# Long differential-attention rows: the first part of the probabilities corrected by two accumulating matmuls with diagonal matrices

## The chip, the cores and the metric

The kernel runs on one core of a Trainium2 chip. TensorE (PE) does the matmuls and the transposes, VectorE (DVE), ScalarE (ACT) and GpSimd (POOL) work element by element, SyncE (SP) issues most of the DMAs. The metric is the device time of one execution in microseconds.

## The reference

One inference step of a two-layer decoder with four parallel mixers in each layer. The change touches the differential attention of the prompt: 2048 tokens, 4 heads, two softmax maps per head whose difference weighs the values.

```python
SEQ = 2048
DEPTH = 2
A_HEADS = 4
Q_BLOCK = 128

def _diff_attend(q1, q2, k1, k2, v, qpos, kpos, lam):
    scale = q1.shape[-1] ** -0.5
    visible = kpos[None, :] <= qpos[:, None]

    def probs(q, k):
        s = jnp.einsum('bqhd,bkhd->bhqk', q.astype(F32), k.astype(F32)) * scale
        return jax.nn.softmax(jnp.where(visible, s, NEG_BIG), axis=-1)

    p = probs(q1, k1) - lam * probs(q2, k2)
    return jnp.einsum('bhqk,bkhd->bqhd', p, v.astype(F32))
...
    o_a = (_rms_norm(o_a, attn_norm_g[l]) * (1.0 - lam_init)).reshape(Bn, T, GROUP_W)
    o_a = o_a * jax.nn.silu(ag.astype(F32))
...
    mixed = jnp.concatenate([o_a, o_b, o_c, o_d], -1).astype(dt) @ w_out[l]
    y = _layer_norm(ALPHA * x + gate[:, None, :] * mixed, ln_g[l], ln_b[l]).astype(dt)
```

## The kernel before

In each layer the projections and the three other mixers come first, then the attention, block by block (tiles 0 to 3, 4 to 7, 8 to 11, 12 and 13, 14 and 15 of 128 queries), with the output projection of finished tiles (`out_tile`, L1326, matmuls L1373 to L1375, 48 per tile) placed among the attention's work.

`attention` (L630) loads keys and queries of one head, and for each tile calls `attn_probs` for it and then `attn_value` for the tile ahead of it, so values run one tile behind. A tile with its head is called a head-tile here.

`attn_probs` (L663) works for the two maps m = 0 and 1 in pieces of up to 1024 keys. For each piece PE makes the scores S (L678, the mask L680), DVE the negated row maximum (L682; in a second piece L684 takes the smaller of the two), ACT the exp into a buffer P with the row sum beside it (L686). Rows of more than 1024 keys (tiles 8 to 15) have two pieces. The first was made with its own maximum, so it needs a correction: a column per map, `col(m, 5)`, from a small exp on ACT (L691). Then DVE forms `r`, the ratio of the two maps' sums times −lambda (L697, L698), and the two maps are joined: P1 + r·P2 for the last piece (L712), and for the first piece of a long row P1·col(0,5) + P2·col(1,5)·r, in three steps: L702 forms the product of the two columns (DVE), L706 scales P2 by it (ACT), L707 scales P1 and adds (DVE). The maps have buffers of their own, P1 five and P2 three.

`attn_value` (L715) turns the joined probabilities in groups of four blocks of 128 keys: four transposes on PE (L725) into a PSUM tile T (of two), a copy to `ph` on ACT (L727, two buffers), four value matmuls (L730) that accumulate in the PSUM tile X. After the last tile of a block X is copied to `asb` (a buffer of its own), turned by L741 and normalised with rows of two `ms` buffers.

The order in which each engine issues its work is not the order of the code. A scheduler that simulates the program sets it, with priorities given by `prio`; any change of an instruction's kind or buffers can therefore move others. The instructions that it moves are shown with the change below.

Of the kernel before, what the change touches and what calls it, by code (L numbers as in the profile page):

```python
# [9 lines left out]
F32 = mybir.dt.float32  # L10
# [4 lines left out]
AF = mybir.ActivationFunctionType  # L15
ALU = mybir.AluOpType
# [8 lines left out]
P = 128  # L25
# [43 lines left out]
def hymba_step_kernel(  # L69
# [9 lines left out]
    nc = tc.nc  # L79
# [9 lines left out]
    RW = TG + NS  # L89
    NB = TG // 512  # L90

    KN = dict(zs=5, ms=2, os=4, NK=5, NMW=8, APO='o k p2 h p1 v v0 op q', ORD0='g10 n1 g2 b4 g4 n1', ORD1='g8 n2',
              NPH=2, NP1=5, NP2=3, LEAD=1, KD0=0, KD1=1, LO0=2, LO1=2, ZIP=0, WF=0, RUN=1, QB=0, RB=0, RC=0, RD=1, RS=1,
              RA=0, RO=0, GP=1, CI=1, CS=0, MO=0, PT=300, PSA=0, PN=1000, PB=0, PG=0, PD=1000, PBV=0, PCZ=0, PGB=0,
              POUT=-500, PATT=0, PMOD=0, PW=0, PAV=0, PDZ=3000, PQK=500, PSL=0, PSLD=0, PPR=0, PPB=0, OT=1, GO=0, DO=0,
              EP2=0, ECB=0, EPH=0, EAS=0, EAV=0, EDV=0, EOH=0, EOL=1, EOT=1, ESH=0, ESL=1, EQK=1, EDN=1, EAN=1, EDB=1,
# [15 lines left out]
    NK, NMW, NPH, NP1, NP2, LEAD = (KN[k] for k in ('NK', 'NMW', 'NPH', 'NP1', 'NP2', 'LEAD'))  # L112
    APO, ORD0, ORD1 = (KN[k].split() for k in ('APO', 'ORD0', 'ORD1'))
# [20 lines left out]
    def nm(s):  # L134
        uid[0] += 1
        return f"{s}_{uid[0]}"
# [14 lines left out]
    def st(tag, dt=F32):  # L151

        return stp.tile([P, 512], dt, tag=tag, name=nm(tag), bufs=NST[tag])
# [46 lines left out]
    ident = cst[:, C_ID:C_ID + 128]  # L200
# [462 lines left out]
    def attn_probs(qi, qt, kst, l1, Lx, ap):  # L663
# [32 lines left out]
        r = col(0, 7)  # L696
        nc.vector.reciprocal(r, lt2)  # L697
        nc.vector.scalar_tensor_tensor(r, lt1, Lx.nlam, r, op0=ALU.mult, op1=ALU.mult)  # L698
        for pc, n in enumerate(sizes):
            p1, p2 = p1s[pc], p2s[pc]  # L700
            if pc == 0 and npc > 1:
                nc.vector.tensor_tensor(col(1, 7), col(1, 5), r, ALU.mult)  # L702
                if KN['EP2']:
                    nc.gpsimd.tensor_scalar(p2[:, :n], p2[:, :n], col(1, 7), None, op0=ALU.mult)
                else:
                    nc.scalar.activation(p2[:, :n], p2[:, :n], AF.Copy, scale=col(1, 7))  # L706
                nc.vector.scalar_tensor_tensor(p1[:, :n], p1[:, :n], col(0, 5), p2[:, :n], op0=ALU.mult, op1=ALU.add)  # L707
            elif n <= KN['ECB'] * P:
                nc.scalar.activation(p2[:, :n], p2[:, :n], AF.Copy, scale=r)
                nc.gpsimd.tensor_tensor(p1[:, :n], p1[:, :n], p2[:, :n], ALU.add)  # L710
            else:
                nc.vector.scalar_tensor_tensor(p1[:, :n], p2[:, :n], r, p1[:, :n], op0=ALU.mult, op1=ALU.add)  # L712
        return p1s

    def attn_value(qi, pm, vst, acc, ls, j4, nt, hd, act, Lx, l, ap):  # L715

# [1 line left out]
        hs = slice(hd * 64, (hd + 1) * 64)  # L718
        for c in range(0, nk, 4):
            n = min(4, nk - c)  # L720
            p1 = pm[c // 8]
            o = (c % 8) * P
            pt = Tt()
            for j in range(n):
                nc.tensor.transpose(pt[:, j * P:(j + 1) * P], p1[:, o + j * P:o + (j + 1) * P], ident)  # L725
            ph = ap.h.tile([P, 4, P], F32, tag="ph", name=nm("ph"), bufs=NPH)
            (nc.vector.tensor_copy if n <= KN['EPH'] else nc.scalar.copy)(ph[:, 0:n].rearrange("p k q -> p (k q)"), pt[:, 0:n * P])  # L727
            for j in range(n):
                e = (c + j) % 2
                nc.tensor.matmul(acc[e * 64:(e + 1) * 64, j4 * P:(j4 + 1) * P], vst[c // 4][:, j, hs], ph[:, j, :],  # L730
                                 start=(c + j < 2), stop=(c + j >= nk - 2), tile_position=(0, e * 64))
        if nk == 1:
            nc.vector.memset(acc[64:128, 0:P], 0.0)
        if j4 < nt - 1:
            return
        asb = ap.o.tile([P, 512], F32, tag="asb", name=nm("asb"), bufs=1)
        cpy('EAS', asb[:, 0:nt * P], acc[:, 0:nt * P])

        pt = Tt()
# [835 lines left out]
```

## Time and profile before

| | |
|---|---|
| median of 3 runs | 3167.21 us (3165.14 to 3172.83) |
| the profiled execution | 3160.83 us |
| its span | 3159.1 us, mean granted TensorE clock 0.951 |
| PE busy | 2828.0 us, 90% of the span |
| DVE busy | 2235.2 us, 71% |
| ACT busy | 1162.9 us, 37% |
| POOL busy | 960.8 us, 30% |
| long rows, layer 0 and layer 1 | 1182 to 1572 and 2712 to 3108 us |

The shares are means over the whole span. The edited lines run in the two stretches of long rows alone, a quarter of the time, so tables of single stretches say more than the page. A row of such a table gives a stretch, its length, and for each engine busy time and count of instructions, then the granted clock of TensorE (1.00 is full speed), the share of the DMA engines and their GB/s. A matmul's own duration includes its way through the array; the next one starts earlier, so a group's time from start to start is what one costs.

### The profile page before, as it was taken

What the parts mean: (1) busy time and instruction counts of PE and PEld (TensorE: products, weight loads), DVE (VectorE), ACT (ScalarE), POOL (GpSimd) and SP (SyncE); (2) the same over time, 40 slices, a digit from 0 to 9 for tenths busy, and PEclk for the clock granted to TensorE, in tenths of its full rate; (3) what the DMA queues carried; (4) which work ended last, traced back from release to release, by engine and by line L of the source; (5) the groups of instructions that cost most, each with busy time, mean ns of one, the idle gap of its engine ahead of it and who ended that gap; (6) DMA issues with size and microseconds to landing.
All of it is one profiled execution on the core that took longest, in us unless ns stands there. A gap on an engine that the chain in (4) does not pass through costs nothing. (4 is left out here: it accounts for less than half of the span.)

```text
span 3159.1 us, 55749 instructions
## 1 busy us (share of the span) xinstructions
PE 2828.0 (90%) x20888; PEld 2254.7 (71%) x20888; DVE 2235.2 (71%) x5280; ACT 1162.9 (37%) x2452; POOL 960.8 (30%) x1061
## 2 busy tenths in 40 slices
PE   5999989898999798888979999999999988997986
PEld 3888876788876566656668888767888856665665
DVE  2567883367583788879956678833676749898897
ACT  3212223211112666666641112232110146567663
POOL 3344364312011233404253344552120031332232
PEclk8999999899999899989989999999999988998998
DMA  6433544323555754446453335444334355444652
GB/s 237 147 128 108 173 146 154 108 92 128 174 180 203 184 133 112 118 112 166 122 197 111 122 119 192 140 139 124 117 120 140 117 166 123 129 118 108 158 155 67
DMA packets 323263, 441.31 MB, mean 140 GB/s; under 512 B 58704, under 2 KB 207734, under 8 KB 315811
## 3 DMA queue, kind: packets, MB, share of 16 engines
q1 hardware_dynamic: 316850, 420.97, 44.0%
q0 software_dynamic: 6144, 16.79, 1.8%
q8 instruction: 165, 2.70, 0.4%
q14 instruction: 104, 0.84, 0.1%
HBM read 295.80 MB, written 142.05 MB: 139 GB/s over the span
## 5 line engine op out<-in xcount | busy, mean ns | idle before, releaser
L525 PE MATMUL z<-hh,wh 128*128 128x512 f32 (+1 forms) x1440 | 528.4, 367 | 17.1 <-DVE zs L195 9.1
L527 PE MATMUL z<-hh,wl 128*128 128x512 f32 (+1 forms) x1440 | 522.1, 363 | 0.0
L526 PE MATMUL z<-hl,wh 128*128 128x512 f32 (+1 forms) x1440 | 518.6, 360 | 0.0
L516 PE MATMUL z<-wh,hh 128*128 128x256 f32 (+1 forms) x1360 | 399.9, 294 | 16.0 <-ACT wh L110 4.3
L686 ACT ACTIVATE P<-S,stt 128x1024 f32<-128x1024 f32 (+7 forms) x384 | 332.7, 868 | 182.1 <-DVE stt L682 120.0
L518 PE MATMUL z<-wh,hl 128*128 128x256 f32 (+1 forms) x1360 | 394.7, 290 | 0.0
L517 PE MATMUL z<-wl,hh 128*128 128x256 f32 (+1 forms) x1360 | 393.9, 290 | 0.6 <-POOL wl L172 0.6
L682 DVE TENSOR_REDUCE stt<-S 128x1 f32<-128x1024 f32 (+7 forms) x384 | 344.0, 904 | 64.2 <-PE S L680 48.7
L1026 DVE SCALAR_TENSOR_TENSOR acc<-glu,cw,acc 128x512 f32<-128x512 f32 x480 | 378.0, 834 | 3.3
L525 PEld LDWEIGHTS z<-hh,wh 128*128 128x128 f32 x1440 | 275.7, 191 | 80.1 <-issue 14.4
L527 PEld LDWEIGHTS z<-hh,wl 128*128 128x128 f32 x1440 | 275.5, 191 | 44.7 <-issue 7.0
L526 PEld LDWEIGHTS z<-hl,wh 128*128 128x128 f32 x1440 | 275.7, 191 | 42.7 <-issue 6.3
L678 PE MATMUL S<-K,Q 128*128 128x512 f32 (+3 forms) x640 | 229.2, 430 | 77.1 <-ACT P L686 61.6
L516 PEld LDWEIGHTS z<-wh,hh 128*128 128x128 f32 (+1 forms) x1360 | 262.3, 193 | 25.9 <-issue 5.7
L517 PEld LDWEIGHTS z<-wl,hh 128*128 128x128 f32 (+1 forms) x1360 | 261.9, 193 | 4.9 <-issue 2.6
L518 PEld LDWEIGHTS z<-wh,hl 128*128 128x128 f32 (+1 forms) x1360 | 261.5, 192 | 2.3 <-issue 0.3
L172 POOL TENSOR_TENSOR wl<-raw,wh 128x512 fp32r<-128x512 f32 x112 | 150.8, 1362 | 256.5 <-ACT wh L110 218.2
L1373 PE MATMUL z<-woh,zs 128*128 128x512 f32 (+1 forms) x480 | 202.7, 422 | 24.0 <-ACT zs L110 15.1
L1375 PE MATMUL z<-woh,zs 128*128 128x512 f32 (+1 forms) x480 | 200.2, 417 | 10.0 <-POOL zs L172 9.8
L730 PE MATMUL X<-ph,V 128*64 128x128 f32 x2176 | 196.1, 294 | 10.4 <-ACT ph L727 9.8
L678 PEld LDWEIGHTS S<-K,Q 128*128 128x128 f32 x640 | 114.9, 204 | 122.1 <-ACT P L686 90.0
L725 PE MATMUL T<-cst,P 128*128 128x128 f32 x1088 | 189.2, 302 | 13.3 <-DVE P L707 8.8
(374 smaller groups left out, 5410.5 us busy)
## 6 DMA issues: line engine op xcount, KB each, us to landing
wp<-wh SPq DMA_DIRECT2D x28, 1024.0 KB
wp<-wl SPq DMA_DIRECT2D x28, 1024.0 KB
wh<-wp SPq DMA_DIRECT2D x56, 512.0 KB
wl<-wp SPq DMA_DIRECT2D x56, 512.0 KB
K<-kh SPq DMA_DIRECT2D x224, 128.0 KB
K<-kl SPq DMA_DIRECT2D x224, 128.0 KB
mw<-in_w_ada_dram SPq DMA_DIRECT2D x24, 1024.0 KB
raw<-in_w_in_dram SPq DMA_DIRECT2D x64, 256.0 KB
```

The lines of the kernel that those rows point to most:

```text
L516: nc.tensor.matmul(ps, hh[:, k, tok:tok + M], wh[:, k, :], start=(k == 0), stop=False)
L517: nc.tensor.matmul(ps, hh[:, k, tok:tok + M], wl[:, k, :], start=False, stop=False)
L518: nc.tensor.matmul(ps, hl[:, k, tok:tok + M], wh[:, k, :], start=False, stop=(k == KT - 1))
L525: nc.tensor.matmul(ps, wh[:, k, ms], hh[:, k, c0:c0 + n], start=(k == 0), stop=False)
L526: nc.tensor.matmul(ps, wh[:, k, ms], hl[:, k, c0:c0 + n], start=False, stop=False)
L527: nc.tensor.matmul(ps, wl[:, k, ms], hh[:, k, c0:c0 + n], start=False, stop=(k == KT - 1))
L678: nc.tensor.matmul(s[:, o:o + w], qt[:, m, :], kst[pc * 2 + o // 512][:, m, 0:w], start=True, stop=not diag)
L682: nc.vector.tensor_reduce(col(m, pc), s[:, :n], AX.X, ALU.max, negate=True)
L686: nc.scalar.activation(p[:, :n], s[:, :n], AF.Exp, bias=col(m, pc), scale=1.0, accum_out=l1 if m == 0 and npc == 1 else col(m, 2 + pc))
L1026: nc.vector.scalar_tensor_tensor(av, src(j), Lx.cw[:, c, j:j + 1], av, op0=ALU.mult, op1=ALU.add)
L1373: nc.tensor.matmul(po[0:M], a, wh[:, k, :], start=(i == 0), stop=False)
L1375: nc.tensor.matmul(po[0:M], b, wh[:, k, :], start=False, stop=(i == KT - 1))
```

## The change

For the first piece of a long row the three passes L702, L706 and L707 are gone. Instead `attn_probs` makes two 128x128 diagonal matrices from the identity, one with col(0,5) and one with col(1,5)·r on the diagonal, in a buffer `dg` (two of them), and hands P1, P2 and `diag` to `attn_value`. There each transpose of the first eight blocks becomes two fp32 matmuls into the same part of T: P1's block times the first diagonal matrix, P2's block times the second, accumulated. Since a block is the stationary operand, the product comes out turned as before. The first piece of P2 is thus read by PE and no longer by ACT and DVE. `asb` becomes an `ms` buffer, which leaves room for the matrices. A branch for very short rows that no row took is gone too.

```diff
-    KN = dict(zs=5, ms=2, os=4, NK=5, NMW=8, APO='o k p2 h p1 v v0 op q', ORD0='g10 n1 g2 b4 g4 n1', ORD1='g8 n2',
+    KN = dict(zs=5, ms=2, os=4, NK=5, NMW=8, APO='o k p2 h p1 v v0 op q dg', ORD0='g10 n1 g2 b4 g4 n1', ORD1='g8 n2',
...
+        diag = None
         for pc, n in enumerate(sizes):
             p1, p2 = p1s[pc], p2s[pc]
             if pc == 0 and npc > 1:
-                nc.vector.tensor_tensor(col(1, 7), col(1, 5), r, ALU.mult)
-                if KN['EP2']:
-                    nc.gpsimd.tensor_scalar(p2[:, :n], p2[:, :n], col(1, 7), None, op0=ALU.mult)
-                else:
-                    nc.scalar.activation(p2[:, :n], p2[:, :n], AF.Copy, scale=col(1, 7))
-                nc.vector.scalar_tensor_tensor(p1[:, :n], p1[:, :n], col(0, 5), p2[:, :n], op0=ALU.mult, op1=ALU.add)
-            elif n <= KN['ECB'] * P:
-                nc.scalar.activation(p2[:, :n], p2[:, :n], AF.Copy, scale=r)
-                nc.gpsimd.tensor_tensor(p1[:, :n], p1[:, :n], p2[:, :n], ALU.add)
+                diag = ap.dg.tile([P, 2, P], F32, tag="dg", name=nm("dg"), bufs=2)
+                nc.vector.tensor_scalar(diag[:, 0], ident, col(0, 5), None, op0=ALU.mult)
+                nc.vector.tensor_scalar(diag[:, 1], ident, col(1, 5), r, op0=ALU.mult, op1=ALU.mult)
             else:
                 nc.vector.scalar_tensor_tensor(p1[:, :n], p2[:, :n], r, p1[:, :n], op0=ALU.mult, op1=ALU.add)
-        return p1s
+        return p1s, p2s, diag
...
-            p1 = pm[c // 8]
+            p1s, p2s, diag = pm
             o = (c % 8) * P
             pt = Tt()
             for j in range(n):
-                nc.tensor.transpose(pt[:, j * P:(j + 1) * P], p1[:, o + j * P:o + (j + 1) * P], ident)
+                ks, js = slice(o + j * P, o + (j + 1) * P), slice(j * P, (j + 1) * P)
+                if diag is not None and c < 8:
+                    for m, p in enumerate((p1s[0], p2s[0])):
+                        nc.tensor.matmul(pt[:, js], p[:, ks], diag[:, m], start=(m == 0), stop=(m == 1))
+                else:
+                    nc.tensor.transpose(pt[:, js], p1s[c // 8][:, ks], ident)
...
-        asb = ap.o.tile([P, 512], F32, tag="asb", name=nm("asb"), bufs=1)
+        asb = st("ms")
```

In the rows of the order below, a name with its numbers is one tile of that name, and what stands behind the arrow is read. After the change the code's lines are shifted: L724 are the paired matmuls, L726 the transposes that stay (L725 before), L731 the value matmuls (L730), L742 the turning of the head's sum (L741), L708 the last piece's combination (L712), L1355 the turning in `out_tile` (L1354) and L1374 to L1376 the output projection (L1373 to L1375).

PE, in a long head-tile of layer 0, before the change: scores of one tile, transposes and value matmuls of the tile ahead (T the transposed blocks, X the value sum).

```order
L680 MATMUL S_1893_12986<-cmaskb_110,identb_108 128x128
L741 MATMUL T_1865_12882<-cst_81,asb_1864_12880 128x64 x4
L1354 MATMUL z_2089_13859<-cst_81,os_2085_13854 128x128 x4
L730 MATMUL X_1874_12914<-ph_1885_12957,V_1189_10171 64x128 x4
L725 MATMUL T_1888_12974<-cst_81,P_1853_12822 128x128
L725 MATMUL T_1886_12963<-cst_81,P_1851_12815 128x128 x4
L678 MATMUL S_1895_12995<-K_1844_12789,Q_1847_12804 128x512
L678 MATMUL S_1895_12995<-K_1845_12794,Q_1847_12804 128x512
L730 MATMUL X_1874_12914<-ph_1887_12968,V_1406_10944 64x128 x4
L725 MATMUL T_1899_13016<-cst_81,P_1877_12920 128x128 x4
L730 MATMUL X_1874_12914<-ph_1889_12976,V_1707_12206 64x128
```

The P tiles that L725 reads here are joined ones: one transpose per block, in groups of four, with score and value matmuls between the groups.

PE, the corresponding part of a long head-tile of layer 0 after the change (dg the diagonal matrices, P read from both maps in turn).

```order
L731 MATMUL X_1884_12981<-ph_1898_13043,V_1407_10947 64x128 x4
L731 MATMUL X_1884_12981<-ph_1900_13051,V_1708_12209 64x128
L678 MATMUL S_1906_13070<-K_1853_12848,Q_1856_12863 128x512
L678 MATMUL S_1906_13070<-K_1854_12853,Q_1856_12863 128x512
L724 MATMUL T_1911_13091<-dg_1894_13015,P_1887_12987 128x128
L678 MATMUL S_1908_13076<-K_1855_12858,Q_1856_12863 128x384
L680 LDWEIGHTS identb_108
L680 MATMUL S_1908_13076<-cmaskb_110,identb_108 128x128
L724 MATMUL T_1911_13091<-dg_1894_13015,P_1891_13002 128x128
L724 MATMUL T_1911_13091<-dg_1894_13015,P_1887_12987 128x128
L724 MATMUL T_1911_13091<-dg_1894_13015,P_1891_13002 128x128
```

The eight transposes of a first piece are sixteen matmuls now, two per block with P of the one map and of the other, and the next tile's scores (L678) stand among them.

DVE, at the last long tile of layer 1 before the change, from the reciprocal to the first piece's combination (stt the columns, the small rows in between belong to normalisations).

```order
L697 RECIPROCAL stt_5208_32157<-stt_5208_32157 128x1
L179 TENSOR_SCALAR smai_5203_32139<-sma_5201_32134 128x2
L189 SCALAR_TENSOR_TENSOR smoa_5290_32524<-smoa_5290_32524,smoy_5289_32523 128x1
L698 SCALAR_TENSOR_TENSOR stt_5208_32157<-ls_5179_32041,nlam_2721_16683,stt_5208_32157 128x1
L181 TENSOR_SCALAR smay_5204_32140<-smai_5203_32139 128x2
L190 SCALAR_TENSOR_TENSOR smoy_5289_32523<-smoa_5290_32524,smoy_5289_32523 128x1
L702 TENSOR_TENSOR stt_5208_32157<-stt_5208_32157 128x1
L712 SCALAR_TENSOR_TENSOR P_5212_32170<-P_5216_32186,stt_5208_32157,P_5212_32170 128x1024
L183 TENSOR_TENSOR smaa_5205_32141<-sma_5201_32134,smay_5204_32140 128x2
L1385 SCALAR_TENSOR_TENSOR smo_5287_32520<-omv_5285_32517,smoy_5289_32523 128x1
L707 SCALAR_TENSOR_TENSOR P_5210_32162<-P_5210_32162,stt_5208_32157,P_5214_32178 128x1024
```

L702 and L707 enclose the last piece's combination L712, and L706 runs on ACT between them.

DVE, at the same tile after the change.

```order
L693 SCALAR_TENSOR_TENSOR stt_5273_32660<-stt_5273_32660 128x1
L189 SCALAR_TENSOR_TENSOR smaa_5270_32644<-smaa_5270_32644,smay_5269_32643 128x2
L697 RECIPROCAL stt_5273_32660<-stt_5273_32660 128x1
L190 SCALAR_TENSOR_TENSOR smay_5269_32643<-smaa_5270_32644,smay_5269_32643 128x2
L698 SCALAR_TENSOR_TENSOR stt_5273_32660<-ls_5243_32536,nlam_2754_16943,stt_5273_32660 128x1
L183 TENSOR_TENSOR smaa_5270_32644<-sma_5266_32637,smay_5269_32643 128x2
L706 TENSOR_SCALAR dg_5282_32695<-cst_81,stt_5273_32660 128x128
L708 SCALAR_TENSOR_TENSOR P_5277_32673<-P_5281_32689,stt_5273_32660,P_5277_32673 128x1024
```

The pass over 1024 columns that read P twice (L707) and the column product ahead of it (L702) are gone, the matrix with `r` (L706) stands between L698 and the last piece's combination; the other matrix stands earlier.

PE, at the end of layer 1 before the change: the last value matmuls, the turning of the last head, and the output projection (z and S its sums).

```order
L730 MATMUL X_5207_32156<-ph_5230_32265,V_4336_28336 64x128 x4
L730 MATMUL X_5207_32156<-ph_5232_32276,V_4737_30098 64x128 x4
L741 MATMUL T_5234_32284<-cst_81,asb_5233_32282 128x64 x2
L1354 MATMUL z_5302_32568<-cst_81,act_5038_31424 128x128
L1373 MATMUL S_5303_32574<-woh_3987_26875,zs_5299_32559 128x512
L1374 MATMUL S_5303_32574<-wol_3988_26876,zs_5299_32559 128x512
L1375 MATMUL S_5303_32574<-woh_3987_26875,zs_5300_32560 128x512
L1373 MATMUL S_5303_32574<-woh_3987_26875,zs_5299_32559 128x512
L1374 MATMUL S_5303_32574<-wol_3988_26876,zs_5299_32559 128x512
L1375 MATMUL S_5303_32574<-woh_3987_26875,zs_5300_32560 128x512
```

Nothing of the output projection is left ahead of the last head's L741 here; what follows belongs to the last two tiles.

PE, at the same place after the change.

```order
L731 MATMUL X_5272_32659<-ph_5298_32795,V_4787_30489 64x128 x4
L1355 MATMUL z_5338_32955<-cst_81,os_5334_32950 128x128 x4
L742 MATMUL T_5300_32803<-cst_81,ms_5299_32801 128x64 x2
L1374 MATMUL z_5346_32976<-woh_4021_27138,zs_5336_32952 128x512
L1375 MATMUL z_5346_32976<-wol_4022_27139,zs_5336_32952 128x512
L1376 MATMUL z_5346_32976<-woh_4021_27138,zs_5337_32953 128x512
L1374 MATMUL z_5346_32976<-woh_4021_27138,zs_5336_32952 128x512
```

Before, the last value matmul is followed by what the last two tiles still need of the output projection, 78 matmuls; after, by 144 of them, those of three whole tiles.

## Rows read from the trace of the kernel before

**Rows 1.** Table by stage: long rows and the ends of both layers (columns as described above).

```profile
1182.00:1572.00 390.00, 336.42 (x2059) 245.22 (x2061) 336.58 (x814) 251.05 (x524) 119.78 (x91) 0.95 0.50 127
1572.00:1622.00 50.00, 37.89 (x194) 27.52 (x191) 32.19 (x111) 16.05 (x31) 19.26 (x16) 0.80 0.55 176
2712.00:3108.00 396.00, 345.64 (x2142) 252.18 (x2140) 353.59 (x849) 257.52 (x535) 126.99 (x97) 0.95 0.50 131
3108.00:3159.00 51.00, 31.61 (x176) 23.13 (x174) 31.65 (x84) 12.15 (x21) 7.53 (x6) 0.83 0.16 54
```

**Rows 2.** Table of two 50 us windows: late short rows, middle of the long rows.

```profile
2680.00:2730.00 50.00, 48.31 (x314) 36.29 (x313) 46.20 (x123) 31.40 (x67) 14.95 (x12) 0.97 0.51 128
1330.00:1380.00 50.00, 38.61 (x260) 26.90 (x258) 40.04 (x107) 39.84 (x85) 5.69 (x5) 0.87 0.42 98
```

**Rows 3.** Chain of waits over the long rows of layer 1, shares by line.

```profile
by line: DVE stt L682 10.9%; PE T L725 7.5%; PE X L730 7.3%; PE z L1375 6.9%; PE z L1373 6.7%; PE S L678 6.5%; PE z L1374 6.2%; issue 4.0%; DVE P L707 3.9%; ACT P L686 3.8%; DVE P L712 3.1%; DVE stt L684 2.3%; SPq L166 2.1%; DMA K<-kl 2.0%;
```

**Rows 4.** Layer 0's long rows by line: form, count | busy us, mean ns | idle before.

```profile
L707 DVE SCALAR_TENSOR_TENSOR P<-P,stt,P 128x1024 f32<-128x1024 f32 x31 | 43.0, 1386 | 3.3 <-ACT P L706 3.2
L706 ACT ACTIVATE P<-P,stt 128x1024 f32<-128x1024 f32 x31 | 35.7, 1151 | 8.8 <-DVE stt L702 8.8
L702 DVE TENSOR_TENSOR stt<-stt 128x1 f32<-128x1 f32 x32 | 9.8, 306 | 0.4
```

**Rows 5.** Whole span by line, DVE: the nearest forms to the added products.

```profile
L1024 DVE TENSOR_SCALAR acc<-hcs,cw,vT 128x64 f32<-128x64 f32 x4 | 1.1, 319 | 0.0
L712 DVE SCALAR_TENSOR_TENSOR P<-P,stt,P 128x128 f32<-128x128 f32 x16 | 6.6, 414 | 0.1
```

**Rows 6.** Timeline of PE and of its weight loads (start us, us, line, form, count).

```profile
1361.46 1.09 PE L725 MATMUL T<-cst,P 128*128 128x128 f32 x8
1363.57 0.66 PE L730 MATMUL X<-ph,V 128*64 128x128 f32 x8
...
251.56 0.30 PEld L1237 LDWEIGHTS T<-Sbd,dq 128*128 128x128 f32 x2
251.77 0.53 PEld L1240 LDWEIGHTS T<-di,attF 128*128 128x128 f32 x4
252.22 0.30 PEld L1242 LDWEIGHTS S<-di,ckE 128*128 128x128 f32 x2
...
251.56 0.49 PE L1237 MATMUL T<-Sbd,dq 128*128 128x128 f32 x2
```

**Rows 7.** Costliest groups of the page: value matmuls and transposes, whole span.

```profile
L730 PE MATMUL X<-ph,V 128*64 128x128 f32 x2176 | 196.1, 294 | 10.4 <-ACT ph L727 9.8
L725 PE MATMUL T<-cst,P 128*128 128x128 f32 x1088 | 189.2, 302 | 13.3 <-DVE P L707 8.8
```

**Rows 8.** Timeline of PE, the last two matmuls of the output projection.

```profile
3145.95 0.39 PE L1374 MATMUL S<-wol,zs 128*128 128x512 f32 x1
3146.18 0.39 PE L1375 MATMUL S<-woh,zs 128*128 128x512 f32 x1
```

**Rows 9.** Layer 1's long rows by line, PE.

```profile
L1373 PE MATMUL z<-woh,zs 128*128 128x512 f32 x195 | 82.2, 421 | 6.7 <-ACT zs L110 4.5 <-DVE t L1377 2.0
L678 PE MATMUL S<-K,Q 128*128 128x512 f32 x172 | 67.4, 457 | 21.0 <-ACT P L686 19.7 <-DMA K<-kl 0.6
L730 PE MATMUL X<-ph,V 128*64 128x128 f32 x768 | 65.3, 289 | 2.0 <-ACT ph L727 1.8
L725 PE MATMUL T<-cst,P 128*128 128x128 f32 x377 | 62.5, 295 | 4.6 <-DVE P L707 4.4
```

**Rows 10.** The dense window 2680 to 2730 by line: one of three alike.

```profile
L1373 PE MATMUL z<-woh,zs 128*128 128x512 f32 x31 | 12.7, 409 | 0.0
```

**Rows 11.** Timeline of PE at the end of layer 1.

```profile
3116.18 1.46 PE L730 MATMUL X<-ph,V 128*64 128x128 f32 x16
...
3122.86 0.48 PE L1354 MATMUL z<-cst,act 128*128 128x128 f32 x1 [4.10 <-DVE act L754]
```

**Rows 12.** Timeline: ACT's exp into P2 and PE's first transposes, layer 1.

```profile
2880.90 0.58 ACT L686 ACTIVATE P<-S,stt 128x384 f32<-128x384 f32 x1 [1.02 <-DVE stt L684]
...
2880.96 1.91 PE L725 MATMUL T<-cst,P 128*128 128x128 f32 x8
```

## What the change does to the time, predicted

> **What bounds the kernel now.** I first looked for the stretches in which the edited lines run: the first pieces of rows longer than 1024 keys, tiles 8 to 15, four heads, two layers, so 8 × 4 × 2 = 64 head-tiles. They fill 1182 to 1572 us and 2712 to 3108 us, 786 us in all. The table by stage [rows 1] says that no engine is full there: PE is busy 336 + 346 = 682 us (87%), DVE 337 + 354 = 690 us (88%), ACT 251 + 258 = 509 us (65%). PE and DVE stand level, so what is taken from DVE and paid for on PE has to be weighed on both.
>
> Next I asked how full PE can get beside attention. Late in the short rows a 50 us window has PE at 48.3 us, 97%, with DVE at 92%; a window in the middle of the long rows has PE at 77%, DVE and ACT at 80% [rows 2]. That middle is limited by hand-overs: scores (PE), maximum (DVE), exp (ACT), combination (ACT, DVE), transposes (PE). No output projection stands in it, while the dense window is filled with it.
>
> The chain of waits over layer 1's long rows [rows 3] names the maximum L682 10.9%, transposes L725 7.5%, value products L730 7.3%, the projection's L1373 to L1375 19.8% together, and the combination L707, which goes, 3.9%: 0.039 × 396 = 15 us.
>
> **The change part by part.**
>
> *Removed from DVE:* L707 at 1.386 us and L702 at 0.306 [rows 4], 1.69 × 64 = 108 us. *Added:* two 128x128 products of the identity with columns. Neither form occurs before. L1024's 128x64 with two columns, half as wide, takes 0.319; the 128x128 combination with a second full operand 0.414 [rows 5]. Between these ends two cost 0.64 to 0.83 us; I take 0.74, the middle, as both rows are near: 47 us. Net on DVE −61 us (−55 to −67).
>
> *Removed from ACT:* L706 at 1.151 us [rows 4] × 64 = −74 us. ACT is 65% busy, so this mostly shortens the way from the last exp to the first transpose: L702, L706 and L707, 2.84 us, become one product of 0.4.
>
> *PE, the transposes.* Eight transposes per head-tile become sixteen plain fp32 matmuls. A transpose steps at (1.09 − 0.3) / 7 = 0.11 us, eight in a row less the last one's own 0.3 [rows 6]. What does a plain fp32 matmul step at? Here counts matter. `attn_value` issues one value matmul for each transpose, yet the page has 2176 records of L730 to 1088 of L725 [rows 7]: a plain fp32 matmul leaves two records, a transpose one. So in the nearest products with a full 128x128 weight, L1237 (128 columns, the first of a sum) and L1240 (64 columns, added onto it), the loads x2 and x4 are one and two matmuls: from 251.56 to 251.77 one, 0.21, and to 252.22 three in 0.66 us, **0.22 each**, twice a transpose [rows 6]. The adding onto a sum is in that figure, so it is the lower bound and the value I take. The upper is L1237's own width, 0.49 less half a matmul's 0.11 for the overlap with the next, 0.38 [rows 6]; it stands alone behind another kind of work, the loads go on evenly, so I stay low. 16 × 0.22 − 8 × 0.11 = 2.64 us a head-tile, **+169 us** on PE; at 0.38 it would be +333.
>
> The Trainium skill, page "TensorE: Matmul & The Clock Gate", section "Terms", has transpose mode four times faster for FP32 on this chip. The rows show a factor of two, 0.22 to 0.11 [rows 6], and I go by them; the other factor is a rival below.
>
> *PE, the order.* By the order of instructions 78 matmuls of the output projection stood behind the last value product of each layer; now 144 do, and the long rows lose 135 over both layers. One steps at 0.23 us at full clock [rows 8], so 31 us leave the long rows.
>
> *PE, need.* Busy time counts the last matmul's way through the array, which the next can cover, so I also add up steps. Layer 1's long rows: the projection's 3 × 195 and the 172 scores of 512 columns at 0.23, 377 transposes at 0.11, 768 value records at 0.056 [rows 6, 9], and some 25 us of smaller ones: 135 + 40 + 41 + 43 + 25 = 284 us, 72% of 396. Layer 0 comes to 272. Together 556, after the change 556 + 169 − 31 = **694 us**. The dense window by the same sum (93 projections [rows 10], 18 scores, 53 transposes, 104 value records, smaller ones): 21.4 + 4.1 + 5.8 + 5.8 + 5 = 42 of 50 us, 84%.
>
> *The layers' ends.* In layer 1 the last value products start at 3116.18 and take 1.46; the last head's turn comes 4.10 us after its L741 [rows 11], and 78 matmuls follow until 3146.18 [rows 8]. Now 66 are ready at once: 3117.6 + 66 × 0.23 = 3132.8, then 78 × 0.23 = 17.9, to 3150.7: 4 us later, +6 with these tiles' evictions (0 to 12). Layer 0's end has 50 − 37.9 = 12 us of idle PE [rows 1], which mostly takes in 66 more: +2 (0 to 10). The last tile's longer matmuls (+2.6) and its shorter combination (−2.4) cancel. Sum +8.
>
> *One answer.* The matrices' pool (two buffers, each read for one head-tile), the head's sum in an `ms` buffer (one per head), later loads of V's first block and some Q on SP: 0 (0 to +2), covered by the time between heads.
>
> *P2's ring.* P2 has three buffers and a long tile takes two, so the exp into the next tile's second P2 piece needs this tile's first piece back. L707 let it go; now the sixteen matmuls do. At 2880.90 that exp starts 0.06 us ahead of this tile's transposes [rows 12]. The matmuls can start some 2.4 us earlier than the transposes did and last 2.6 longer, so they end about when those ended. In 26 of 62 neighbouring pairs the exp started sooner than that, by 87 us in all. ACT's idle third can take much of it; I leave it to the density below and to the rivals.
>
> **The sum.** PE's need of 694 us in 786 would be 88%, more than the dense window's 84%, and PE is now the fuller engine: DVE has 690 − 61 = 629, less some 16 of evictions that move out. At 84% the long rows take 826 us (+40), at 90% 771 (−15). I take 85%, just above the window, since DVE at 92% there comes to some 75% here: 816 us, +30. With +8 at the ends +38. The profiled execution took 3160.83 us (span 3159.1), so 3198.8; the median stands 6.4 above it (3167.21): **3205 us**, slower.
>
> **The rivals.**
>
> *A: DVE and the combination's way were the limit (faster).* If PE packs at 92% once they are shorter, the long rows take 754 us, −32, with +8 −24: 3143. It decides from 694 / (786 − 8) = 89% on. For it: the way from exp to transpose is 2.4 us shorter, the new order has projection between all long heads to fill PE, and PE is 97% busy in the dense window [rows 2]. Against: its need there is 84% only. Chance 0.14.
>
> *B: the two cancel (about the same).* At 88 to 90%: 789 to 771, +3 to −15, with the ends +11 to −7: 3160 to 3178. Chance 0.18.
>
> *C: the added matmuls lie on the chain (slower still).* L725's 7.5% of 396 is 30 us, of which by the tiles' first parts some 20; with four times the PE time that is +60, less L707's 15 and a few of L702's, +43 a layer. Two layers +86, less half of the projection's 31, with +8 at the ends: +78, 3245. P2's ring works the same way. For it: [rows 3, 12]. Against: the scheduler has put scores between the matmuls, so the chain need not keep its way. Chance 0.18.
>
> *D: the step is another.* At one record per matmul (0.11) PE's need is 694 − 113 = 581, no more than now, and DVE's gain is left: −32 at 754 us, 3140; chance 0.05. At four times a transpose (0.44) it is 694 + 225 = 919, at 85% 1081, +295: 3470; chance 0.02, as the whole run of loads in [rows 6] is half of that.
>
> **How the numbers follow.** My forecast (84 to 87%) has 0.43. About 0.3% (10 us) is what a measurement of this kernel can tell from no change. Slower: forecast, C and D's dear end, 0.63; same: B, 0.18; faster: A and D's cheap end, 0.19. The range goes from 3143 (A) to 3250 (C, with 5 us for the unpriced loads and ends); below it lie some 0.1, above it 0.07.
>
> **What would show it.** Right: two records for each paired matmul, 0.11 apart; PE over 90% busy in the long rows, DVE near 615 to 630 us, ACT less by 74; long rows of some 816 us; layer 1's end about 48 us behind its last value product, not 43. Wrong: long rows under 771 us (A); idle time at L686 ended by the paired matmuls of over 30 us (C); a step of 0.11 or 0.44 (D). What undoes the sum most easily is the density: one per cent of it is 9 us.

## The result and the profile after

The change makes the kernel slower: the median is 3245.55 us (3235.18 to 3253.38) against 3170.02 us (3165.14 to 3173.24), a ratio of 1.0238 with a 95% interval of 1.0203 to 1.0272. In a second set of runs, on another chip, the ratio was 1.0229 (1.0186 to 1.0271). The forecast was slower by 1.2%: the direction came right and the time lies in the stated range, but the slowdown was twice as large as forecast. The profiled execution took 3235.18 us, with a span of 3233.2.

The busy times of the page, engine by engine (time, share of the span, instructions):

```profile
span 3233.2 us, 58783 instructions
PE 2979.9 (92%) x22424; PEld 2426.4 (75%) x22424; DVE 2198.9 (68%) x5280; ACT 1100.0 (34%) x2388; POOL 951.1 (29%) x1061
```

PE has 152 us more than before, DVE 36 less, ACT 63 less, and the span has grown by 74. The table by stage of the kernel after, in the stretches that answer to [rows 1]: long rows of layer 0, its end, long rows of layer 1, its end (length, then busy time of PE, weight loads, DVE, ACT, POOL, then the granted clock):

```profile
1182.00:1572.00 390.00, 381.34 (x2758) 307.18 (x2755) 309.32 (x803) 220.87 (x494) 97.93 (x81) 1.00 0.46 119
1572.00:1651.00 79.00, 57.34 (x278) 42.42 (x276) 44.59 (x119) 16.88 (x32) 37.55 (x29) 0.83 0.54 174
2765.00:3156.00 391.00, 382.78 (x2783) 308.26 (x2783) 313.06 (x808) 223.38 (x500) 99.81 (x83) 1.00 0.47 120
3156.00:3233.00 77.00, 58.60 (x300) 44.85 (x299) 46.77 (x124) 15.63 (x28) 25.57 (x19) 0.89 0.29 89
```

Two things are to be seen here. The long rows take as long as before, 390 and 391 us against 390 and 396, with PE at 98% instead of 87% and its clock at 1.00 instead of 0.95. And the ends, 50 and 51 us before, take 79 and 77.

The paired matmuls in the page's list of groups (first row: matmuls, second: weight loads), and one run of them on PE's timeline with its neighbours:

```profile
L724 PE MATMUL T<-dg,P 128*128 128x128 f32 x2048 | 272.0, 280 | 7.9 <-DVE dg L706 7.9
L724 PEld LDWEIGHTS T<-dg,P 128*128 128x128 f32 x2048 | 248.9, 192 | 28.1 <-issue 14.1
```

```profile
1391.51 0.23 PE L680 MATMUL S<-cmaskb,identb 128*128 128x128 bf16 x1
1391.58 3.57 PE L724 MATMUL T<-dg,P 128*128 128x128 f32 x30
1394.90 0.71 PE L678 MATMUL S<-K,Q 128*128 128x512 f32 x2
```

1024 matmuls leave 2048 records, and 30 of these take 3.57 us, (3.57 − 0.28) / 29 = 0.113 apart: 0.23 us a matmul, as worked out from [rows 6, 7]. PE waits for the matrices 7.9 us in the whole span. The two products that make them, from the list by line of layer 0's long rows, cost 0.457 + 0.388 = 0.85 us a head-tile:

```profile
L705 DVE TENSOR_SCALAR dg<-cst,stt 128x128 f32<-128x128 f32 x31 | 14.2, 457 | 0.0
L706 DVE TENSOR_SCALAR dg<-cst,stt 128x128 f32<-128x128 f32 x31 | 12.0, 388 | 0.4
```

To place the loss I cut the attention of each layer at five events of the trace: its first score, the first exp of a long row, its last score, its last value product, and the first matmul of the next layer's L460 (in layer 1 the end of the span). Times in us, in brackets the output projection's matmuls that start in the piece:

| layer, piece | before | after | difference |
|---|---|---|---|
| 0, short rows | 137.8 (142) | 138.8 (120) | +1.0 |
| 0, long rows | 400.0 (574) | 399.0 (504) | −1.0 |
| 0, last value products | 15.6 (20) | 24.5 (46) | +8.9 |
| 0, end | 39.3 (78) | 59.7 (114) | +20.4 |
| 1, short rows | 127.7 (95) | 140.5 (110) | +12.8 |
| 1, long rows | 402.6 (613) | 396.8 (504) | −5.8 |
| 1, last value products | 14.1 (18) | 24.6 (46) | +10.5 |
| 1, end | 41.7 (78) | 57.7 (144) | +16.0 |

The sum is +63 us of 74; the other 11 lie in front of layer 1's attention, where 30 of layer 0's matmuls run between layer 1's first ones (the last at 1661.0, L460's first at 1651.0). Behind the last score stand 92 more matmuls of the projection in layer 0 and 94 in layer 1: 186 × 0.23 = 43 us at full clock. With the longer matmuls of the last two tiles of each layer (4 × 2.6 = 10 us) that is 53 of the 67 us that these pieces and the 11 us make up. Most of the other 14 are idle time of PE in layer 0's end: 21 us of 60 after the change, 11 of 39 before, at much the same clock, 0.77 and 0.74. The two stretches, before and after, and what PE waited for after:

```profile
1582.80:1621.80 39.00, 27.70 (x101) 20.15 (x98) 25.43 (x77) 9.17 (x19) 16.35 (x14) 0.74 0.62 200
1591.40:1651.00 59.60, 38.89 (x145) 27.92 (x139) 35.26 (x106) 12.35 (x24) 31.43 (x24) 0.77 0.63 202
```

```profile
PE T L395 <- DVE vT L349: 4.5, 1, 4.5
PE z L1355 <- DVE smo L1384: 4.3, 1, 4.3
PE T L421 <- DVE smp L365: 4.1, 1, 4.1
PE T L421 <- DVE Z L417: 2.1, 1, 2.1
PE T L412 <- DVE cw L396: 2.0, 1, 2.0
```

L395, L412 and L421 are small transposes that prepare weights of the next layer. They stand ahead of most of what is left of the projection in PE's order and wait 12.7 us for DVE; before the change L395 waited 3.0 us and the other two did not. A smaller part is clock: the timeline shows some of the projection's matmuls 0.43 us apart instead of 0.23, 43 of them in both ends together, 29 before, some 3 us more:

```profile
1614.52 0.77 PE L1374 MATMUL z<-woh,zs 128*128 128x512 f32 x1
1615.09 0.63 PE L1375 MATMUL z<-wol,zs 128*128 128x512 f32 x1
1615.52 0.63 PE L1376 MATMUL z<-woh,zs 128*128 128x512 f32 x1
```

So the long rows paid for the pairs in another coin: they kept their length and gave up 179 matmuls of the projection (70 and 109), most of which then had to run behind them.

### The profile page after: what moved, and what is told of

Same layout as the page of the kernel before. It is cut to its first block, busy times and chain, and to the rows that moved or that the text cites. A ratio compares the mean times of both kernels' runs of the same rounds, so it can differ in the third digit from the quotient of the medians.

```text
span 3233.2 us, 58783 instructions
## 1 busy us (share of the span) xinstructions
PE 2979.9 (92%) x22424; PEld 2426.4 (75%) x22424; DVE 2198.9 (68%) x5280; ACT 1100.0 (34%) x2388; POOL 951.1 (29%) x1061
## 5 line engine op out<-in xcount | busy, mean ns | idle before, releaser
L686 ACT ACTIVATE P<-S,stt 128x1024 f32<-128x1024 f32 (+7 forms) x384 | 333.1, 869 | 227.1 <-DVE stt L682 157.9
L724 PE MATMUL T<-dg,P 128*128 128x128 f32 x2048 | 272.0, 280 | 7.9 <-DVE dg L706 7.9
L724 PEld LDWEIGHTS T<-dg,P 128*128 128x128 f32 x2048 | 248.9, 192 | 28.1 <-issue 14.1
L678 PE MATMUL S<-K,Q 128*128 128x512 f32 (+3 forms) x640 | 224.2, 422 | 24.9 <-ACT P L686 17.7
L728 ACT COPY ph<-T 128x512 f32<-128x512 f32 (+2 forms) x320 | 162.2, 522 | 207.3 <-PE T L726 104.5
L1374 PE MATMUL z<-woh,zs 128*128 128x512 f32 (+1 forms) x480 | 200.3, 417 | 14.3 <-ACT zs L110 9.8
L731 PE MATMUL X<-ph,V 128*64 128x128 f32 x2176 | 200.0, 294 | 3.0 <-ACT ph L728 2.6
```

The lines of the kernel that those rows point to most:

```text
L678: nc.tensor.matmul(s[:, o:o + w], qt[:, m, :], kst[pc * 2 + o // 512][:, m, 0:w], start=True, stop=not diag)
L686: nc.scalar.activation(p[:, :n], s[:, :n], AF.Exp, bias=col(m, pc), scale=1.0, accum_out=l1 if m == 0 and npc == 1 else col(m, 2 + pc))
L724: nc.tensor.matmul(pt[:, js], p[:, ks], diag[:, m], start=(m == 0), stop=(m == 1))
L1374: nc.tensor.matmul(po[0:M], a, wh[:, k, :], start=(i == 0), stop=False)
```

## The experiments

Two theories to begin with. **PE work is paid in full**: the pairs' 169 us are more than PE can take in, wherever the projection stands. **Order**: the scheduler's new order, with 144 instead of 78 of the projection's matmuls behind the last value product, is what costs, and the work itself would fit. A third, **waits**, has the place of the pairs in the hand-overs (P2's buffers) as the cause. Ratios below are against the kernel before on the same chip; the chips' medians of it ranged from 3170 to 3194 us, so medians of different sets are not compared. Attention pieces of traces are, with care: in the two traces of the kernel after, from two chips, they sum to 1242 and 1245 us.

### Transposes alone in the kernel after

```diff
-                if diag is not None and c < 8:
-                    for m, p in enumerate((p1s[0], p2s[0])):
-                        nc.tensor.matmul(pt[:, js], p[:, ks], diag[:, m], start=(m == 0), stop=(m == 1))
-                else:
+                if True:
```

> The kernel after, but the first eight blocks are turned by single transposes of P1 again: the part of P2 in the first 1024 keys of long rows and both of its corrections are left out of the sum, the two diagonal matrices are still made. PE has no added work, DVE and ACT keep their savings. Theory 'PE work is paid in full' (the 169 us of added matmuls are what costs; nothing idle takes them in): faster than before, 3100 to 3150 us, with 78 projection matmuls behind the last value product. Rival 'order' (the projection pushed to the ends is what costs): the ends are as before, so about the same time, 3100 to 3150, too; it does not tell these two apart but gives the worth of the savings alone. Rival 'waits' (the shorter combination buys nothing, since other hand-overs hold the rows): 3155 to 3175.

Measured: 0.9931 (0.9901 to 0.9962). Without the pairs the change would have been a gain of 0.7%: the removed passes are worth something, though L707 made only 3.9% of the chain [rows 3]. The strong form of 'waits', that nothing is gained at all, is out. The run can't part the pairs' work from their place in the hand-overs, since P2's first piece is not read at all in it.

### The pairs alone in the kernel before

```diff
+    zero = cp.tile([P, 128], F32, name="zero")
+    nc.vector.memset(zero, 0.0)
...
-                nc.tensor.transpose(pt[:, j * P:(j + 1) * P], p1[:, o + j * P:o + (j + 1) * P], ident)
+                if long and c < 8:
+                    for m, p in enumerate((p1s[0], p2s[0])):
+                        nc.tensor.matmul(pt[:, js], p[:, ks], (ident, zero)[m], start=(m == 0), stop=(m == 1))
+                else:
+                    nc.tensor.transpose(pt[:, js], p1[:, ks], ident)
```

> The kernel before with all of its corrections on DVE and ACT, and beside them paired plain fp32 matmuls in place of the transposes of the first eight blocks, against the identity and against a matrix of zeros: PE has the 169 us more, DVE and ACT save nothing. 'PE work is paid in full': 3240 to 3300 us, as slow as the kernel after or slower. 'Order': only 78 to 90 projection matmuls stand behind the last value products, so 3170 to 3200.

Measured: 1.0262 (1.0227 to 1.0297). With 90 and 78 matmuls of the projection behind the last value products, almost as before, the loss is there in full. (Behind the last scores there are 132 and 131, against 98 and 96: at 0.23 us that is 16 of the 83 us.) Nor do P2's buffers explain it: in its trace the exp waits 1.3 us in all for a paired matmul. Its long rows, from the table by stage, are longer instead, 426 and 422 us, with PE at 95 and 97%:

```profile
1184.00:1610.00 426.00, 403.96 (x2841) 322.35 (x2842) 346.37 (x828) 261.19 (x538) 109.74 (x89) 0.97 0.46 119
2784.00:3206.00 422.00, 408.76 (x2876) 325.11 (x2876) 353.14 (x852) 263.05 (x540) 122.67 (x95) 0.99 0.48 123
```

### One plain matmul per block

```diff
-                    for m, p in enumerate((p1s[0], p2s[0])):
-                        nc.tensor.matmul(pt[:, js], p[:, ks], diag[:, m], start=(m == 0), stop=(m == 1))
+                    for m, p in enumerate((p1s[0],)):
+                        nc.tensor.matmul(pt[:, js], p[:, ks], diag[:, m], start=True, stop=True)
```

> The kernel after with one plain fp32 matmul per block instead of two, P1 against its diagonal matrix; the part of P2 in the first 1024 keys is left out. PE gets 8 x 0.22 - 8 x 0.11 = 0.88 us a head-tile, 56 us in all instead of 169. 'PE work is paid in full': a third of the way from the run with transposes alone to the kernel after, 3150 to 3185 us. 'Order': 118 projection matmuls stand behind the last value products, 40 of the 66 more, so some 45 us over before, 3205 to 3220.

Measured: 0.9993 (0.9966 to 1.0020). A third of the added PE time gives back the gain of the run with transposes and no more, although 118 matmuls stand behind the last value products. 'Order' had asked for 1.4% more. From here to the kernel after the other 113 us of PE time cost another 2.4%, some 75 us. That a larger part is paid the more PE is filled is not shown by this: P2's first piece, unread here, is read again in that step, and the run with rounded operands below, of the same dose, lies 0.9% higher.

### The projection brought back into the rows

```diff
-              POUT=-500, PATT=0, PMOD=0, PW=0, PAV=0, PDZ=3000, PQK=500, PSL=0, PSLD=0, PPR=0, PPB=0, OT=1, GO=0, DO=0,
+              POUT=0, PATT=0, PMOD=0, PW=0, PAV=0, PDZ=3000, PQK=500, PSL=0, PSLD=0, PPR=0, PPB=0, OT=1, GO=0, DO=0,
```

> The kernel after with one number changed: the output projection has no lowered priority, so 78 of its matmuls stand behind the last value products as before, not 144. Same work on every engine. 'PE work is paid in full': the ends get shorter and the long rows longer by as much, 3230 to 3255 us. 'Order': the ends cost what they did before, 3175 to 3195.

Measured: 1.0283 (1.0241 to 1.0326), not faster than the kernel after, if anything slower. The table by stage (long rows and end of each layer):

```profile
1190.00:1615.00 425.00, 412.45 (x2875) 327.35 (x2874) 333.72 (x846) 229.88 (x510) 125.94 (x100) 0.99 0.47 121
1615.00:1678.00 63.00, 50.12 (x273) 37.83 (x274) 33.82 (x121) 18.19 (x38) 19.43 (x16) 0.84 0.49 150
2789.00:3219.00 430.00, 413.18 (x2871) 327.98 (x2870) 336.30 (x846) 229.38 (x509) 122.50 (x98) 0.99 0.47 121
3219.00:3283.00 64.00, 44.53 (x265) 34.18 (x265) 32.68 (x112) 14.82 (x30) 7.53 (x6) 0.87 0.18 58
```

The ends are short again (cut at the events above 41.2 and 41.8 us, as before), and the long rows have grown by 26 and 33 us. Behind each layer's last score stand 105 matmuls here, close to the 98 and 96 before, so 'order' has fallen: the scheduler's choice to push the projection out cost nothing against this one.

### Rounded operands for the pairs

```diff
-                nc.scalar.activation(p[:, :n], s[:, :n], AF.Exp,
+                nc.scalar.activation((p.bitcast(F32R) if pc == 0 and npc > 1 else p)[:, :n], s[:, :n], AF.Exp,
...
-                diag = ap.dg.tile([P, 2, P], F32, tag="dg", name=nm("dg"), bufs=2)
+                diag = ap.dg.tile([P, 2, P], F32R, tag="dg", name=nm("dg"), bufs=2)
...
-                        nc.tensor.matmul(pt[:, js], p[:, ks], diag[:, m], start=(m == 0), stop=(m == 1))
+                        nc.tensor.matmul(pt[:, js], p.bitcast(F32R)[:, ks], diag[:, m], start=(m == 0), stop=(m == 1))
```

> The kernel after with its paired matmuls in the one-record form: the first pieces of long rows and the diagonal matrices are written as fp32r, which rounds them. Same instructions, same order of work, waits and buffers; each matmul leaves one record, whose step should be about 0.06 us instead of 0.22, so sixteen cost what the eight transposes did. 'PE work is paid in full': like the run with transposes alone, 0.990 to 0.996 of the kernel before. Rival 'waits' (the pairs' place in the hand-overs, P2's buffers among them, costs, not their length): 1.01 to 1.02.

Measured: 1.0081 (1.0053 to 1.0108). My step was wrong. One record per matmul came, but on the timeline a run of 14 takes 1.68 us, (1.68 − 0.28) / 13 = 0.108 each, no less than a record of the plain form:

```profile
1404.21 1.68 PE L724 MATMUL T<-dg,P 128*128 128x128 f32 x14
```

So the dose is 16 × 0.108 − 8 × 0.11 = 0.85 us a head-tile, about that of the single matmuls, 0.88. It still cost 0.9% more than those, with attention pieces that sum to 1180 us against 1176 there (on two chips). P2's buffers, read by the pairs here and not there, do not show as the cause: no exp waits for a paired matmul. What differs is the clock: the mean granted clock of this kernel's executions was 0.940, of the kernel before on the same chip 0.947; with single matmuls it was 0.948 against 0.945. Why it was lower I have not found. With the pairs' PE time halved two thirds of the loss are gone. Not all else was kept, as I had expected it to be: 84 and 78 of the projection's matmuls stand behind the last value products here, not 144.

### No correction at all

```diff
-                nc.vector.tensor_reduce(col(m, pc), s[:, :n], AX.X, ALU.max, negate=True)
-                if pc:
-                    nc.vector.tensor_tensor(col(m, pc), col(m, pc), col(m, 0), ALU.min)
+                if not pc:
+                    nc.vector.tensor_reduce(col(m, pc), s[:, :n], AX.X, ALU.max, negate=True)
...
-                nc.scalar.activation(p[:, :n], s[:, :n], AF.Exp, bias=col(m, pc), scale=1.0, accum_out=l1 if m == 0 and npc == 1 else col(m, 2 + pc))
+                nc.scalar.activation(p[:, :n], s[:, :n], AF.Exp, bias=col(m, 0), scale=1.0, accum_out=l1 if m == 0 and npc == 1 else col(m, 2 + pc))
...
-                nc.scalar.activation(col(m, 5), col(m, 0), AF.Exp, bias=col(m, 1), scale=-1.0)
...
-                nc.vector.scalar_tensor_tensor(lt, col(m, 2), col(m, 5), col(m, 3), op0=ALU.mult, op1=ALU.add)
+                nc.vector.tensor_tensor(lt, col(m, 2), col(m, 3), ALU.add)
...
-            if pc == 0 and npc > 1:
+            if False:
```

> The kernel before, made without the correction instead of moving it: the second piece of a long row takes the first piece's maximum as its bias, so both pieces have one scale and are joined by L712's step alone; the second piece's maximum, the small exp and the columns' product go. It is the same function as long as no later score passes the first 1024 keys' maximum by some 88. DVE loses about 96 us of maxima and 20 of small steps (126 in all with the dropped products), ACT 74 + 37, PE gets nothing. 'PE work is paid in full' (gains on DVE and ACT count where PE is not asked for more): 0.975 to 0.985 of the kernel before. If PE's own 87% already held the rows: 0.99 to 1.0.

Measured: 0.9913 (0.9882 to 0.9945), median 3136.74 us. It beats both kernels, at the price of a narrower range of scores. The gain of 0.9% is less than half of the 2% in the middle of what I expected. Its long rows take 360 and 362 us with PE at 90 and 91%, but the last value products 27 us in each layer, because 60 of the projection's matmuls stand among them: here, too, PE's work that leaves the rows comes back behind them.

```profile
1180.00:1540.00 360.00, 323.82 (x2089) 238.73 (x2085) 296.02 (x659) 209.05 (x440) 123.06 (x87) 0.96 0.53 138
2695.00:3057.00 362.00, 328.89 (x2119) 240.64 (x2118) 302.56 (x679) 208.91 (x439) 134.06 (x91) 0.98 0.55 140
```

### The sum's buffer, and where the pools lie

```diff
-        asb = ap.o.tile([P, 512], F32, tag="asb", name=nm("asb"), bufs=1)
+        asb = st("ms")
```

> The kernel before with one part of the change alone: the head's sum copy in an ms buffer instead of its own, which also moves the pools and with them the loads of V's first block and of two heads' Q. I priced that part at 0 to 2 us. Expected 0.998 to 1.002; if this part is what makes layer 1's short rows 12 us longer in the kernel after, 1.003 to 1.005, with those rows near 140 us.

Measured: 1.0064 (1.0039 to 1.0088). A part that I had priced at nothing costs 0.6%. Without `asb` every pool behind `o` lies 2 KB lower, and the first loads of Q are issued 795 us into the run, against 586 in the kernel before. Given three `ms` buffers instead of two this kernel would have the instructions of PE, DVE, ACT and POOL in the same order, which speaks against the ring; there is no run of it. Three runs test whether it is the placement. First the same edit with the room of `asb` kept:

```diff
+        pad = ap.o.tile([P, 512], F32, tag="asb", name=nm("pad"), bufs=1)
+        asb = st("ms")
```

> The kernel before with the head's sum in an ms buffer, as in the run with that part alone, but with the old buffer still reserved and not used, so that no pool moves. 'Placement': 0.998 to 1.002 of the kernel before, and layer 1's short rows near 128 us. 'Ms ring': 1.005 to 1.009, those rows near 150 us as in the run without the reserve.

Measured: 0.9973 (0.9952 to 0.9995). The loss is gone, and the first loads of Q are issued at 599 us. The attention pieces of both layers sum to 1168 us here and to 1189 in the run without the reserve. It is not the way I thought, though: layer 1's short rows take 142 us here too (150 without the reserve, 128 in the kernel before), and the difference is spread over the rest. In all of these runs the first loads of Q are issued over 200 us ahead of the first score, so how the shift costs time is open. In the run without the reserve the loss goes with a lower mean granted clock, 0.941 against 0.947 of the kernel before on the same chip; with the room kept it is 0.943 against 0.943. Then the matrices' pool in that room, in the kernel after and in the one with transposes alone:

```diff
-    KN = dict(zs=5, ms=2, os=4, NK=5, NMW=8, APO='o k p2 h p1 v v0 op q dg', ORD0='g10 n1 g2 b4 g4 n1', ORD1='g8 n2',
+    KN = dict(zs=5, ms=2, os=4, NK=5, NMW=8, APO='o dg k p2 h p1 v v0 op q', ORD0='g10 n1 g2 b4 g4 n1', ORD1='g8 n2',
```

> The kernel after with the matrices' pool named second instead of last, in the room that the head's sum left, so that the pools behind it keep their addresses. The loads of Q for the first two heads and of V's first block then stand where they stood before the change. Nothing else is changed. Theory 'placement' (what the run with the sum's buffer alone lost, 0.6%, comes from shifted pools, which make these loads wait for other buffers and turn the order of the short rows): 1.014 to 1.020 of the kernel before. Rival 'ms ring' (the sum shares two buffers): unchanged, 1.020 to 1.028.

> The run with transposes of P1 alone (the part of P2 in the first 1024 keys of long rows and its corrections left out), with the matrices' pool in the second place. 'Placement': 0.984 to 0.990 of the kernel before, against 0.993 with the pool in the last place. 'Ms ring': 0.991 to 0.996. It also gives the worth of the savings on DVE and ACT with nothing else moved.

> The kernel after, unchanged, on the same chip as the three others, so that they are compared with it too: 1.020 to 1.028 of the kernel before by both theories.

Measured, on one chip: 1.0183 (1.0144 to 1.0222) for the kernel after with the pool in second place, 1.0229 (1.0186 to 1.0271) for the kernel after itself, and 0.9901 (0.9876 to 0.9926) for transposes alone. The point values go the way of 'placement', but the intervals of the first two overlap and their attention pieces differ by 6 us only (1239 and 1245). So placement is shown to cost in the kernel before (0.9% between the two runs with the sum in `ms`); how much of the change's own 2.4% it makes is open, by these intervals between nothing and some 1%.

The long rows of transposes alone, with no pool moved, show what the savings do: 377 and 386 us against 400 and 403, PE at 90 and 89%.

```profile
1181.00:1558.00 377.00, 338.70 (x2180) 247.47 (x2179) 323.42 (x859) 228.74 (x513) 121.45 (x99) 0.98 0.53 139
2712.00:3098.00 386.00, 344.61 (x2146) 252.26 (x2146) 328.47 (x844) 228.86 (x511) 118.96 (x96) 0.95 0.51 133
```

**What they add up to.** With the matrices' pool in the second place the savings on DVE and ACT give −1.0%, and the pairs on top of them +2.8% (1.0183 − 0.9901), some 90 us for 169 us of PE time; in the kernel before the pairs alone give +2.6%, 83 us. 'PE work is paid in full' was too strong as well: about half of it is paid. The other half goes where PE had been idle or at its lower clock: in the long rows PE was 87% busy at a mean clock of 0.95 before, 98% at 1.00 after.

P2's ring, my rival C, is not seen. The waits of the exp L686 over layer 1's long rows after the change (total us, times, longest) name DVE's maximum and small steps, and no paired matmul:

```profile
ACT P L686 <- DVE stt L682: 48.5, 36, 4.8
ACT P L686 <- DVE stt L684: 24.6, 21, 3.7
ACT P L686 <- DVE smaa L183: 8.9, 2, 4.8
```

## Why the prediction was right in direction and half in size

Of the forecast's +38 us the long rows were to bring +30 and the layers' ends +8. By the cut above the long rows brought −7, what stands behind the last scores +67 and the short rows +14. With the density as it came and the ends as forecast, the same sum would have ended near rival B, no change. So the mechanism held in its first half, PE gets more work than it can take in, and failed in where that is paid; that two terms were off in opposite ways and left the right sign is in part luck.

- **Records and step of the pairs: right.** Two records each, 0.11 apart, +169 us on PE, as taken from [rows 6, 7]. The counts did it: at one record per matmul the same rows would have given a third of that, and a gain (the cheap end of rival D).
- **DVE and ACT: near.** The matrices cost 0.85 us a head-tile in layer 0's long rows, a little above my upper bound of 0.83 (0.74 taken). DVE's long rows came to 622 us, within the 615 to 630 that I named, but on the page DVE fell by 36 us where I had summed −61. ACT's busy time fell by 63 us in the span where L706 had taken 74. "Neither form occurs before" was wrong: a product with two columns on 128x128 stood in the kernel before, at 0.407 us, and two of it are 0.81.

```profile
L474 DVE TENSOR_SCALAR zs<-S,sc1T,shT 128x128 f32<-128x128 f32 x32 | 12.4, 407 | 8.9 <-PE S L460 7.7 <-DMA Q<-qh 0.4
```

- **The long rows: mis-sized, too dear.** I took a density of 85% and +30 us; in the stretches of the table by stage they changed by 0 and −5. PE's need came out as summed. By the same steps layer 0's 390 us hold 490 matmuls of the projection and 170 scores at 0.23, 989 pair records at 0.113, 133 transposes at 0.11, 762 value records at 0.056 and 25 us of smaller ones: 113 + 39 + 112 + 15 + 43 + 25 = 346 us; layer 1's 391 hold 348. That is 694 us, the predicted figure, in 781: 89%, at a clock of 1.00. My densest window, 84%, had a clock of 0.97 and DVE at 92% [rows 2], and by the cut above 29 of its 50 us lie in the long rows, not in the short ones; it was no upper bound. By the same steps the pairs alone in the kernel before come to 85% (725 of 848 us) and the kernel with the projection brought back to 86% (735 of 855): that is my density, in rows that keep most of their projection. The kernel after gave away 179 of its matmuls, where I had counted 135. Two rows by line of layer 0's stretch stand for these counts:

```profile
L724 PE MATMUL T<-dg,P 128*128 128x128 f32 x989 | 131.6, 280 | 3.3 <-DVE dg L706 3.3
L1375 PE MATMUL z<-wol,zs 128*128 128x512 f32 x163 | 65.6, 403 | 0.0
```

- **The layers' ends: the step that failed.** I gave them +8 us. The pieces behind the last score grew by 29 and 26.5 us, and 11 more spilled into layer 1's start: 67 us. I had counted 66 matmuls behind the last *value product* of each layer, and let the wait of 4.10 us [rows 11] and layer 0's 12 us of idle PE [rows 1] take most of them in. But 92 and 94 more stand behind the last *score*, and the idle time did not take them in. Layer 0's end has 21 us of it instead of 11, by the waits shown above. In layer 1's, ahead of the last matmul, 7 us became 5: the wait of 4.10 is down to 0.52, but PE waits for other operands, 1.21 us for ACT and 0.58 for POOL right behind the last head, and runs part of the matmuls at half clock (a granted clock of 0.68 over the first 9.5 us). The timeline of PE in layer 1's end:

```profile
3175.14 0.66 PE L731 MATMUL X<-ph,V 128*64 128x128 f32 x8
3176.05 0.66 PE L1355 MATMUL z<-cst,os 128*128 128x128 f32 x4 [0.25 <-DVE t L1378]
3176.55 0.56 PE L742 MATMUL T<-cst,ms 128*128 128x64 f32 x4
3178.31 0.50 PE L1374 MATMUL z<-woh,zs 128*128 128x512 f32 x1 [1.21 <-ACT zs L110]
3178.65 0.46 PE L1375 MATMUL z<-wol,zs 128*128 128x512 f32 x1
3179.69 0.80 PE L1376 MATMUL z<-woh,zs 128*128 128x512 f32 x1 [0.58 <-POOL zs L172]
```

  The end of layer 1 took 57.7 us instead of 41.7: 16 more for 66 more matmuls, 66 × 0.23 = 15: there they were paid in full. The "last tile's longer matmuls and shorter combination cancel" was wrong too: with PE full behind the last score only the longer matmuls count.
- **"One answer", priced at 0 to 2 us: wrong.** The sum's buffer by itself cost 0.6% in the kernel before, and nothing with the old buffer's room kept. I had seen the later loads on SP and left them at nothing because the time between heads seemed to cover them.
- **Short rows of layer 1: not in my sum**, +12.8 us. 15 more matmuls of the projection stand there (3.5 us), and the granted clock is 0.84 instead of 0.88; why the clock is lower there I did not settle.
- **Rivals.** A and B did not come; C's size came, but not by its mechanism. D's dear end, a step of four transposes (0.44 us), is refuted by the rows: 0.23 against 0.11. The Trainium skill's page "TensorE: Matmul & The Clock Gate", section "Terms", has that factor of four for FP32; this trace shows two.

## What to carry to other kernels

Count the records of a matmul against the calls in the code before you price it, and price the dearer engine's added work at the place where the work that it pushes out will run. A stretch can keep its length and still lose, when filler that used to run in it comes back behind it, where nothing hides it and the clock is lower. A buffer that changes its pool can move every pool behind it, which cost 0.6% here: run that part by itself before calling it free.

## What the runs showed of the hardware

Matmuls of 128 columns with a full 128x128 weight stood 0.11 us a record apart both in plain fp32 (two records each) and with operands written as fp32r (one record, 0.108 us), where I had expected half of it. With PE at 98% busy the granted clock of the long rows stood at 1.00, against 0.95 with PE at 86 and 87% before the change; but the run with rounded operands had 0.95 at 94 and 93%.
